# Low parts of weight tiles by accumulating transfers, in the plain stage of a two-layer decoder trunk

## The chip, the cores and the metric

The kernel runs on one core of a Trainium2 chip. The metric is the time of one execution on the device in microseconds (us). Of the kernel before, three timed runs are shown; their median is 888.7 us. A profiled execution of the same program gives the rows that are quoted here: for each engine when an instruction started, how long it took and what ended the idle time ahead of it. The engines are called as the profile calls them: PE is the matrix engine's multiplying, PEld its loading of weights, DVE the vector engine, ACT the scalar engine, POOL the general engine (GpSimd), SP the engine that here only issues transfers. POOL can issue transfers too.

## The reference

Two layers over 512 tokens of width 1024, in float32. Layer 0 mixes tokens with causal means over 2, 4, 8 and 16 tokens, layer 1 with sliding-window attention. Behind each mixer stands a gated MLP with a causal convolution of width 3 over the tokens:

```python
def conv_glu_ffn(h, w_in, conv_w, conv_b, w_out):
    u = h @ w_in
    c = lax.conv_general_dilated(u, conv_w[:, None, :], window_strides=(1,),
        padding=[(CONV_W - 1, 0)], dimension_numbers=('NWC', 'WIO', 'NWC'),
        feature_group_count=2 * D_FF) + conv_b
    a, g = c[..., :D_FF], c[..., D_FF:]
    return (a * jax.nn.silu(g)) @ w_out
```

D_FF is 2816, so w_in is 1024 by 5632. RMS norms stand ahead of mixers and MLPs and at the end.

## The kernel before, in words

Every product of float32 matrices is made of three products of a shorter format, float32r: an operand x is split into a high part, x rounded to float32r, and a low part, the rest x - high, also float32r; high by high, high by low and low by high are added up in one accumulation bank. `mm3` (lines 89 to 91) issues the three. For a weight tile of 128 by 1024, `weights` (line 98 on) fetches the raw tile by SP, makes the high part by an ACT copy (line 105) and the low part by a subtraction (line 108), on DVE or, for layer 0's first MLP stage, on POOL in four pieces of 256 columns. Raw tiles lie in a ring of three buffers, high and low parts in rings of four each; a fetch waits until the last reader of the buffer three tiles ago is through, a split until PE has finished with the tile four ago.

The program begins with products of zeros on PE (`warm`, line 257), while the first inputs arrive. Then come the pooling mixer (line 290: means over tokens as products with a band matrix `sband`, which DVE scales at line 288) and layer 0's MLP, `mlp_halves`. Its 22 blocks of 128 features come in two kinds. The first seven are "plain": for each block j and each side s (1 the gate, 0 the value) one chunk, 24 products of 512 columns on the weight tile wi_j_s, 14 chunks in all. The other 15 blocks, the halves stage, are made with fewer products from sums and differences of weights (`uw_...` tiles: r, u, v and q) and of the two halves of the input (`th`, `tl`), which DVE and ACT prepare during the plain stage (lines 413 to 433). Between their products PE does the down projection piece by piece (`down`), in two banks that take turns; DVE adds each finished piece to h (line 533), and PE may write the bank again only after that.

For a chunk, DVE scales the finished bank (line 395), ACT and DVE make the convolution's three taps (359, 360, 361), ACT the gate's silu (372), DVE the product of gate and value (376), and both split it (390, 391). Chunks' jobs are put off by some chunks and handed out by a short table of letters per chunk. uw_u tiles are summed by a transfer from memory and a second, accumulating one on POOL's queue (line 451); uw_v comes from two POOL sums (487, 488).

Which instruction stands where in an engine's list is set by the tile framework, which orders the recorded work by its own estimate of when things are ready, save where a pin keeps the written order; each engine then works its list strictly in order. `pre` has the first four weight tiles, which are split during the mixer, by `early_weights`. The loop over the remaining twelve chunks starts a tile's load one chunk ahead:

```python
ahead = [load(2)]
for at in range(2, len(todo)):
    w, ps = ahead.pop(0), chunk(at)
    for i in {11: (12, 13), 12: ()}.get(at, (at + 1,)):
        ahead.append(load(i))
```

Of the kernel before, what the change touches and what calls it, by code (L numbers as in the profile page):

```python
# [19 lines left out]
F32 = mybir.dt.float32  # L20
F32R = mybir.dt.float32r
I32 = mybir.dt.int32
AF = mybir.ActivationFunctionType
ALU = mybir.AluOpType
AX = mybir.AxisListType

P = 128
D = 1024
# [34 lines left out]
def trunk(ctx: ExitStack, tc: tile.TileContext, x_tok, x_t, vecs, w_pool, w_kq, w_v, w_o, gain, w_in, w_half, w_down, w_tok, out):  # L63
    nc = tc.nc
    V, A, G, T = nc.vector, nc.scalar, nc.gpsimd, nc.tensor
# [3 lines left out]
    wp = ctx.enter_context(tc.tile_pool(name="wp", bufs=4))  # L69
# [12 lines left out]
    def bank(tag):  # L82
        rings[tag].append(rings[tag].pop(0))
        return banks[rings[tag][-1]]


    def mm3(ps, w, x, start, stop, **kw):
        (wh, wl), (xh, xl) = w, x
        T.matmul(ps, lhsT=wh, rhs=xh, start=start, stop=False, **kw)  # L89
        T.matmul(ps, lhsT=wh, rhs=xl, start=False, stop=False, **kw)  # L90
        T.matmul(ps, lhsT=wl, rhs=xh, start=False, stop=stop, **kw)  # L91

    def fetch(src, n, name):
        raw = wp.tile([P, 1024], F32, tag="raw", name=f"{name}_raw", bufs=3)
        nc.sync.dma_start(raw[:, :n], src)
        return raw
# [3 lines left out]
    def weights(src, n, name, eng=None, raw=None, step=1024, pin=lambda ins: ins):  # L100

        raw = raw or fetch(src, n, name)
        h = wp.tile([P, 1024], F32R, tag="wh", name=f"{name}_h")
        l = wp.tile([P, 1024], F32R, tag="wl", name=f"{name}_l")
        pin(A.activation(h[:, :n], raw[:, :n], AF.Copy))  # L105
        for a in range(0, n, step):
            o = slice(a, min(a + step, n))
            lows.append((eng or V).tensor_tensor(l[:, o], raw[:, o], h[:, o].bitcast(F32), ALU.subtract))  # L108
        return h, l

    def part(w, k, m=P):
        return tuple(t[:, k * m : (k + 1) * m] for t in w)

    def in_weights(layer, j, s, eng=None, raw=None, pin=lambda ins: ins):
        return weights(w_in[layer][j, s], D, f"wi{layer}_{j}_{s}", eng, raw, 256 if eng else 1024, pin)
# [23 lines left out]
    h = [hp[c // 2][:, (c % 2) * S : (c % 2 + 1) * S] for c in range(NC)]  # L139
# [17 lines left out]
    for g, w in enumerate(WINDOWS):  # L157
# [5 lines left out]
        f = band[:, 4 + g, : w - 1]  # L163
# [86 lines left out]
    def pool_mixer(norm, xs, ws):  # L250
# [2 lines left out]

        warm = small(fst, BW, 192, name="warm")
        V.memset(warm, 0.0)
        for i in range(12):
            T.matmul(banks[-1][:, :BW], lhsT=warm[:, :P], rhs=warm, start=True, stop=True)  # L257
        for i in range(NT):

# [2 lines left out]
            if cut < D:  # L262
                for g in range(2):
# [6 lines left out]
                        scale=1.0,  # L270
# [93 lines left out]
    def mlp_halves(fp, xs, norm, ws0, after):  # L364
# [39 lines left out]
        def spread_signs():  # L404
            mx, px = (sm.tile([P, S], F32, tag="sq", name=f"{x}x") for x in "mp")
            A.activation(mx[:, lo], rb[:, lo], AF.Copy, scale=-1.0)
            A.activation(mx[:, hi], rb[:, hi], AF.Copy)
            A.activation(px, mx, AF.Copy, scale=-1.0)
            return mx, px
# [6 lines left out]
        def first_part(p):  # L416
            th.append(fp.tile([P, 7, HS], F32R, tag="th", name=f"th{p}", bufs=4))
            tl.append(fp.tile([P, 7, HS], F32R, tag="tl", name=f"tl{p}", bufs=4))
            y = spare(p, f"ty{p}").bitcast(F32).rearrange("p (a b) -> p a b", a=4)
            ys.append(y)  # L420
            m2, p2 = (blocks(t) for t in signs)
            V.scalar_tensor_tensor(y[:, 0:4:3, :], blocks(h[p]), col(V_NFF + p), m2, ALU.mult, ALU.mult)  # L422
            V.scalar_tensor_tensor(y[:, 1:3, :], blocks(h[p + 4]), col(V_NFF + p + 4), p2, ALU.mult, ALU.mult)
            split_part(y, p, 0, 3)

        def second_part(p):
            y = ys[p]
            v = spare(p + 4, f"tv{p}").bitcast(F32).rearrange("p (a b) -> p a b", a=4)
            tv.append(v)
            V.tensor_tensor(v[:, 0, :], y[:, 3, :], y[:, 2, :], ALU.add)  # L430
            V.tensor_tensor(v[:, 1, :], y[:, 3, :], y[:, 0, :], ALU.add)
            V.scalar_tensor_tensor(v[:, 2, :], y[:, 2, :], -1.0, v[:, 1, :], ALU.mult, ALU.subtract)
            V.tensor_tensor(v[:, 3, :], y[:, 1, :], v[:, 2, :], ALU.subtract)
            split_part(v, p, 3, 7)
# [11 lines left out]
        def fetch_sums(j):  # L446

            src = w_half[j - PLAIN]
            u = us[j] = fp.tile([P, 1024], F32, tag="ur", name=f"uw{j}_u_raw", bufs=2)
            nc.sync.dma_start(blocks(u), src[:, 0:4:2, :])  # L450
            pin(G.dma_start(blocks(u), src[:, 2:4, :], accum_op=ALU.add))

        def fetch_rows(j):

            if j > PLAIN:
                rs[j] = wp.tile([P, 1024], F32, tag="raw", name=f"uw{j}_r_raw", bufs=3)
            else:
                rs[j] = fp.tile([P, 1024], F32R, tag="vh", name=f"uw{j}_r_raw", bufs=3).bitcast(F32)
            nc.sync.dma_start(blocks(rs[j]), w_half[j - PLAIN][:, 0:2, :])
# [3 lines left out]
        def keep():  # L463
            hold.append(tuple(wp.tile([P, 1024], F32R, tag=f"w{k}", name=f"uw_hold{len(hold)}_{k}") for k in "hl"))
# [8 lines left out]
        def first_weights(j):  # L473

            if j > PLAIN:
                q = wp.tile([P, 1024], F32, tag="raw", name=f"uw{j}_q_raw", bufs=3)
            else:
                q = sm.tile([P, S], F32, tag="sq", name=f"uw{j}_q_raw")
            nc.sync.dma_start(q[:, :half], w_half[j - PLAIN][:, 3, :])
            raws[j] = q  # L480
            uw[j] = kept((j - PLAIN) % 2, slice(0, 1024), rs[j]), own_split(us[j], f"uw{j}_u")
# [32 lines left out]
        def down_split(i):  # L514
            if i < len(steps):
                g, m = steps[i]
                n = DOWN0[g] * P
                at, a = (2, half) if i % 3 == 0 else (3, i % 3 * half - half)
                w = kept(at, slice(a, a + n), down_raw.pop(i)[:, :n])
                down_w[i] = [part(w, k) for k in range(DOWN0[g])]  # L520
# [24 lines left out]
        todo = [(j, s) for j in range(PLAIN) for s in (1, 0)]  # L545
        jobs, ends, fetched = [], [], 0

        def work(n=1, *more):
            for x in range(min(n, len(jobs))):
                f, *args = jobs.pop(0)  # L550
                f(*args, *more)

        def load(i):
            if i < len(todo):
                return ws0.pop(0) if ws0 else in_weights(0, *todo[i], G)

        def chunk(i):
            if i == 6:
                rings["ps"][:0] = [6, 7]
            ps = bank("ps")  # L560
            jobs.append((late, *todo[i], ps))
            return ps

        w, pss = [load(i) for i in range(2)], [chunk(i) for i in range(2)]
        for k in range(NC):
            for i in range(2):
                mm3(pss[i], part(w[i], k), xs[k], k == 0, k == NC - 1)
        ahead = [load(2)]
        for at in range(2, len(todo)):
            w, ps = ahead.pop(0), chunk(at)  # L570
            for i in {11: (12, 13), 12: ()}.get(at, (at + 1,)):
                ahead.append(load(i))
            for k in range(NC):
                if at == 3 and k == 3:
                    r = norm.stats(bank("aux"), root=True)
                if at == 3 and k == 6:
                    rb = norm.spread(r)
                    signs = spread_signs()
                mm3(ps, part(w, k), xs[k], k == 0, k == NC - 1)
            for x in {3: "01", 4: "01", 5: "01", 6: "01", 7: "21f", 8: "21f", 9: "21", 10: "21gd", 11: "1rd", 12: "ea", 13: "vg"}.get(at, ""):  # L580
                if x == "0":
                    first_part(len(th))
                elif x == "2":
                    second_part(len(tv))
                elif x == "1":
                    work()
                elif x == "f":
                    fetch_sums(PLAIN + fetched)
                    fetched += 1
                elif x == "r":  # L590
                    keep()
                    keep()
                    hold.insert(1, None)
                    first_weights(PLAIN)
                    down_split(0)
                elif x == "g":
                    fetch_rows(PLAIN + (at > 12))
                elif x == "a":
                    add_weights(PLAIN)
                elif x == "d":  # L600
                    down_fetch(at - 10)
                elif x == "e":
                    work(1, ends)
                else:
                    summed = second_weights(PLAIN, pin)
# [428 lines left out]
    ws0 = []  # L1034
# [7 lines left out]
    with tc.tile_pool(name="ap", bufs=2) as ap:  # L1042
# [150 lines left out]
        todo = work()  # L1193
# [187 lines left out]
```

## Time and profile before

| | us |
|---|---|
| three timed runs | 888.65, 888.7, 890.28 |
| median | 888.7 |
| profiled execution | 889.68 |
| its span, first to last instruction | 887.8 |
| PE busy | 876.8 |
| DVE busy | 703.1 |
| ACT busy | 509.5 |
| POOL busy | 251.9 |

A row of a timeline holds the start, the duration, the engine, the source line, the operation, the tile written and the tiles read, the shape and a count of merged instructions, and, in brackets, the idle time just before with what ended it. A row of a group holds the busy time of all its instructions and the mean of one in ns. A row of stretches holds the busy time of each engine in that stretch. Matrix products overlap: a row's duration is longer than the distance to the next, and the distance is what counts. The plain stage runs from about 27 to 103 us, the halves stage from there to about 350.

### The profile page before, as it was taken

The page shows a single profiled execution, that of the slowest core. Times are in us where ns is not written, and L with a number is a line of the kernel's source. Part 1 is how long each engine was busy: PE and PEld are TensorE (multiplying, and loading weights), DVE is VectorE, ACT ScalarE, POOL GpSimd, SP SyncE. Part 2 cuts the span into 40 slices and gives each one's busy share as a digit, 9 for nine tenths or more (in the row PEclk, how much of TensorE's full clock was granted, in tenths as well). Part 3 has the DMA queues.
Part 4 walks back from the last instruction along what each step waited for, and adds up shares of the span by engine and source line. Part 5 has one row for each costly group of instructions (what it writes and reads, how often), then busy time and mean ns, then how long its engine had stood idle before and what let it go on. Part 6 is the DMA issues. An engine that isn't in the chain of part 4 may idle for free.

```text
span 887.8 us, 12919 instructions
## 1 busy us (share of the span) xinstructions
PE 876.8 (99%) x4720; PEld 760.2 (86%) x4720; DVE 703.1 (79%) x1106; ACT 509.5 (57%) x851; POOL 251.9 (28%) x331
## 2 busy tenths in 40 slices
PE   8999999999999999999999999999999999999996
PEld 8888889999999998888899888888888888888885
DVE  7989998887788885765887386998886777876887
ACT  7856555645455553545888375797633444533644
POOL 4767332221313110345765130000230002200122
PEclk9999999999999999999999999999999999999999
DMA  8444346565555543222110042265386231582423
GB/s 324 143 137 122 109 128 183 152 166 145 145 163 153 133 131 88 80 85 103 52 48 25 1 142 95 99 165 163 77 205 217 95 95 48 118 229 89 133 61 105
DMA packets 38559, 109.98 MB, mean 124 GB/s; under 512 B 4064, under 2 KB 6112, under 8 KB 38496
## 3 DMA queue, kind: packets, MB, share of 16 engines
q1 hardware_dynamic: 34464, 95.26, 33.0%
q0 software_dynamic: 3888, 13.63, 9.3%
q8 instruction: 37, 0.61, 0.3%
q10 hardware_dynamic: 144, 0.26, 0.1%
q14 instruction: 26, 0.21, 0.1%
HBM read 107.04 MB, written 2.10 MB: 123 GB/s over the span
## 4 chain that ended last, share of the span: by engine, by line
PE 87%; DVE 9%; ACT 2%; issue 1%; POOL 0%; ACTq 0%; DVEq 0%
PE bank L89 28%; PE bank L90 28%; PE bank L91 28%; PE bank L1217 1%; PE bank L1245 1%; ACT sc L1233 1%; DVE bank L395 1%; PE bank L290 1%; DVE tl L414 1%; PE bank L257 1%; DVE uw_hold_l L470 1%; DVE a_t L376 1%; DVE a_t L361 0%; DVE g_t L360 0%; DVE ty L422 0%
## 5 line engine op out<-in xcount | busy, mean ns | idle before, releaser
L89 PE MATMUL bank<-f1x_h,wi_h 128*128 128x512 f32 x352 | 137.1, 389 | 0.0
L90 PE MATMUL bank<-f1x_l,wi_h 128*128 128x512 f32 x352 | 136.9, 389 | 0.0
L91 PE MATMUL bank<-f1x_h,wi_l 128*128 128x512 f32 x352 | 136.8, 389 | 0.0
L105 ACT ACTIVATE wi_h<-wi_raw 128x1024 fp32r<-128x1024 f32 x58 | 61.4, 1058 | 59.0 <-PE bank L90 41.0
L108 DVE TENSOR_TENSOR wi_l<-wi_raw,wi_h 128x1024 fp32r<-128x1024 f32 x44 | 53.8, 1222 | 37.3 <-ACT wi_h L105 37.1
L91 PEld LDWEIGHTS bank<-f1x_h,wi_l 128*128 128x128 f32 x352 | 66.1, 188 | 14.0 <-DVE wi_l L108 0.2
L90 PEld LDWEIGHTS bank<-f1x_l,wi_h 128*128 128x128 f32 x352 | 66.1, 188 | 13.7
L89 PEld LDWEIGHTS bank<-f1x_h,wi_h 128*128 128x128 f32 x352 | 66.1, 188 | 13.5
L487 POOL TENSOR_TENSOR uw_r_raw<-uw_r_raw,uw_u_raw 128x512 f32<-128x512 f32 x15 | 25.1, 1670 | 162.6 <-DVE uw_hold_l L470 149.8
L108 POOL TENSOR_TENSOR wi_l<-wi_raw,wi_h 128x256 fp32r<-128x256 f32 x56 | 53.5, 987 | 28.5 <-ACT wi_h L105 28.4
L844 POOL TENSOR_TENSOR wt_a_raw<-wt_a_raw,wt_s_raw 128x1024 f32<-128x1024 f32 (+1 forms) x6 | 13.4, 2235 | 144.6 <-DVE wt_a_l L108 142.3
L91 PE MATMUL bank<-th,uw_hold_l 128*128 128x256 f32 x180 | 50.9, 283 | 0.0
L90 PE MATMUL bank<-tl,uw_hold_h 128*128 128x256 f32 x180 | 50.9, 283 | 0.0
L89 PE MATMUL bank<-th,uw_hold_h 128*128 128x256 f32 x180 | 50.8, 282 | 0.0
L832 POOL DMA_DIRECT2D wt_s_raw<-w_tok x12 | 10.5, 871 | 140.8 <-DMA wt_s_raw<-w_tok 86.8
L222 POOL TENSOR_TENSOR n_acc<-n_acc,n_sq 128x512 f32<-128x512 f32 x13 | 19.1, 1470 | 86.4 <-ACT n_sq L213 86.3
L90 PE MATMUL bank<-f0x_l,wi_h 128*128 128x512 f32 x112 | 43.6, 389 | 0.0
L91 PE MATMUL bank<-f0x_h,wi_l 128*128 128x512 f32 x112 | 43.6, 389 | 0.0
L89 PE MATMUL bank<-f0x_h,wi_h 128*128 128x512 f32 x112 | 43.0, 390 | 0.0
L469 ACT ACTIVATE uw_hold_h<-wo_raw 128x512 fp32r<-128x512 f32 (+1 forms) x48 | 28.4, 591 | 25.3 <-PE bank L90 18.8
L533 DVE TENSOR_TENSOR h<-bank,h 128x512 f32<-128x512 f32 x48 | 32.9, 685 | 11.7 <-PE bank L91 11.4
L689 ACT ACTIVATE c_t<-bank,vec 128x512 f32<-128x512 f32 x44 | 33.4, 766 | 8.3 <-PE bank L91 5.3
(440 smaller groups left out, 2825.3 us busy)
## 6 DMA issues: line engine op xcount, KB each, us to landing
wi_raw<-w_in SPq DMA_DIRECT2D x58, 512.0 KB, 3.3
wo_raw<-w_down SPq DMA_DIRECT2D x32, 256.0 KB, 2.6
uw_u_raw<-w_half SPq DMA_DIRECT2D x15, 512.0 KB, 5.5
uw_u_raw<-w_half POOLq DMA_DIRECT2D x15, 512.0 KB, 5.8
uw_r_raw<-w_half SPq DMA_DIRECT2D x15, 512.0 KB, 3.4
wt_a_raw<-w_tok SPq DMA_DIRECT2D x15, 512.0 KB, 3.9
wt_s_raw<-w_tok SPq DMA_DIRECT2D x11, 512.0 KB, 4.0
kq_raw<-w_kq SPq DMA_DIRECT2D x10, 512.0 KB, 3.2
```

Source lines behind the costliest of these rows:

```text
L89: T.matmul(ps, lhsT=wh, rhs=xh, start=start, stop=False, **kw)
L90: T.matmul(ps, lhsT=wh, rhs=xl, start=False, stop=False, **kw)
L91: T.matmul(ps, lhsT=wl, rhs=xh, start=False, stop=stop, **kw)
L105: pin(A.activation(h[:, :n], raw[:, :n], AF.Copy))
L108: lows.append((eng or V).tensor_tensor(l[:, o], raw[:, o], h[:, o].bitcast(F32), ALU.subtract))
L222: eng.tensor_tensor(self.acc[:, lo:hi], self.acc[:, lo:hi], sq[:, lo:hi], ALU.add)
L469: A.activation(w[0], raw, AF.Copy)
L487: G.tensor_tensor(r[:, :n], r[:, :n], u[:, n:], ALU.add)
L533: V.tensor_tensor(h[m], ps, h[m], ALU.add)
L689: taps.append(A.activation(t, ps, AF.Identity, bias=col(V_CB + layer * 2 * NF + m), scale=cw[2]))
L832: pin(G.dma_start(r[:, :n], src[:, b1, :], accum_op=ALU.add))
L844: G.tensor_tensor(r[:, :n], r[:, :n], raws["s1", s][:, :n], ALU.add)
```

## The change

Three edits. A new function, `landed_weights`, takes the place of `in_weights` for layer 0's tiles from the fifth on (ten tiles: the first four come from `pre`). It fetches the raw tile and makes the high part as before. Then ACT copies the raw tile a second time with scale -1 into the low tile, which rounds it to minus the high part, and a transfer on POOL's queue adds the raw tile to it where it lies, from on-chip memory to on-chip memory. Raw minus high is the low part, as before. The raw buffer is read until that transfer has landed. Second, two tiles are loaded ahead in the loop, and the special cases at 11 and 12 are gone. Third, ten calls with zeros are made at the start where there were twelve; each is two instructions in the profile, so 20 for 24.

```diff
+    def landed_weights(layer, j, t):
+
+        raw = fetch(w_in[layer][j, t], D, f"wi{layer}_{j}_{t}")
+        h = wp.tile([P, 1024], F32R, tag="wh", name=f"wi{layer}_{j}_{t}_h")
+        l = wp.tile([P, 1024], F32R, tag="wl", name=f"wi{layer}_{j}_{t}_l")
+        A.activation(h, raw, AF.Copy)
+        A.activation(l, raw, AF.Copy, scale=-1.0)
+        G.dma_start(l.bitcast(F32), raw, accum_op=ALU.add)
         return h, l
...
-        for i in range(12):
+        for i in range(10):
             T.matmul(banks[-1][:, :BW], lhsT=warm[:, :P], rhs=warm, start=True, stop=True)
...
-                return ws0.pop(0) if ws0 else in_weights(0, *todo[i], G)
+                return ws0.pop(0) if ws0 else landed_weights(0, *todo[i]) if i > 2 else in_weights(0, *todo[i], G)
...
-        ahead = [load(2)]
+        ahead = [load(2), load(3)]
         for at in range(2, len(todo)):
             w, ps = ahead.pop(0), chunk(at)
-            for i in {11: (12, 13), 12: ()}.get(at, (at + 1,)):
-                ahead.append(load(i))
+            ahead.append(load(at + 2))
```

POOL's list in the plain stage, before. The names are wi_j_s, and l, h and raw are the low, high and raw tile; x4 are the four pieces.

```order
L108 TENSOR_TENSOR wi_1_0_l<-wi_1_0_raw,wi_1_0_h 128x256 x4
L108 TENSOR_TENSOR wi_2_1_l<-wi_2_1_raw,wi_2_1_h 128x256 x4
L108 TENSOR_TENSOR wi_2_0_l<-wi_2_0_raw,wi_2_0_h 128x256 x4
L108 TENSOR_TENSOR wi_3_1_l<-wi_3_1_raw,wi_3_1_h 128x256 x4
L108 TENSOR_TENSOR wi_3_0_l<-wi_3_0_raw,wi_3_0_h 128x256 x4
L108 TENSOR_TENSOR wi_4_1_l<-wi_4_1_raw,wi_4_1_h 128x256 x4
L451 DMA uw_u_raw<-w_half 128x1024
L108 TENSOR_TENSOR wi_4_0_l<-wi_4_0_raw,wi_4_0_h 128x256 x4
L451 DMA uw_u_raw<-w_half 128x1024
L108 TENSOR_TENSOR wi_5_1_l<-wi_5_1_raw,wi_5_1_h 128x256 x4
```

The same stretch of POOL's list with the change (the lines below the new function move by ten, or nine):

```order
L108 TENSOR_TENSOR wi_1_0_l<-wi_1_0_raw,wi_1_0_h 128x256 x4
L118 DMA wi_2_1_l<-wi_2_1_raw 128x1024
L118 DMA wi_2_0_l<-wi_2_0_raw 128x1024
L118 DMA wi_3_1_l<-wi_3_1_raw 128x1024
L118 DMA wi_3_0_l<-wi_3_0_raw 128x1024
L118 DMA wi_4_1_l<-wi_4_1_raw 128x1024
L118 DMA wi_4_0_l<-wi_4_0_raw 128x1024
L461 DMA uw_u_raw<-w_half 128x1024
L118 DMA wi_5_1_l<-wi_5_1_raw 128x1024
L461 DMA uw_u_raw<-w_half 128x1024
L118 DMA wi_5_0_l<-wi_5_0_raw 128x1024
```

Forty subtractions have gone and ten transfers stand in their places; the two accumulations of uw_u come one tile later.

ACT's list around the first changed tile, before:

```order
L213 ACTIVATE n_sq_472<-h_98 128x512
L105 ACTIVATE wi_2_1_h<-wi_2_1_raw 128x1024
L213 ACTIVATE n_sq_475<-h_99 128x512
L213 ACTIVATE n_sq_478<-h_99 128x512
L105 ACTIVATE wi_2_0_h<-wi_2_0_raw 128x1024
L105 ACTIVATE wi_3_1_h<-wi_3_1_raw 128x1024
L184 ACTIVATE rs_y<-bank_76,eps 128x16
```

And with the change:

```order
L223 ACTIVATE n_sq_470<-h_98 128x512
L116 ACTIVATE wi_2_1_h<-wi_2_1_raw 128x1024
L223 ACTIVATE n_sq_473<-h_99 128x512
L223 ACTIVATE n_sq_476<-h_99 128x512
L117 ACTIVATE wi_2_1_l<-wi_2_1_raw 128x1024
L116 ACTIVATE wi_2_0_h<-wi_2_0_raw 128x1024
L117 ACTIVATE wi_2_0_l<-wi_2_0_raw 128x1024
L116 ACTIVATE wi_3_1_h<-wi_3_1_raw 128x1024
L117 ACTIVATE wi_3_1_l<-wi_3_1_raw 128x1024
L194 ACTIVATE rs_y<-bank_76,eps 128x16
```

Each tile's negated copy stands behind its high copy, for this tile behind two squares of the norm as well; the high copies keep their places among ACT's other work. In SP's list the fetch of wi_6_1's raw tile now stands behind two fetches of the halves stage (a down-projection tile and a uw_q tile) instead of ahead of them. On DVE one split of uw_u moves up by eight places at the end of the plain stage, and three operations beside it change places; PE's list is the same but for the zeros.

More of the change, by code (lines that the diff above doesn't have):

```diff
@@ L108, in weights @@
             lows.append((eng or V).tensor_tensor(l[:, o], raw[:, o], h[:, o].bitcast(F32), ALU.subtract))
+        return h, l
+    def landed_weights(layer, j, t):
[5 more added lines that the diff above has]
+        G.dma_start(l.bitcast(F32), raw, accum_op=ALU.add)
         return h, l
```

## The prediction

> **What bounds the kernel now.** I read the page first (busy time, chain, groups), then the stretches in which the changed code runs, then the idle time of TensorE by place. The whole kernel is a TensorE program:
>
> ```profile
> span 887.8 us, 12919 instructions
> PE 876.8 (99%) x4720; PEld 760.2 (86%) x4720; DVE 703.1 (79%) x1106; ACT 509.5 (57%) x851; POOL 251.9 (28%) x331
> 60.00:104.00 44.00, 44.00 (x198) 36.53 (x197) 43.93 (x65) 24.66 (x31) 28.04 (x26) 1.00 0.46 128
> ```
>
> PE is busy 876.8 of 887.8 us, so the change can only win what lies in the other 11 us, or what PE spends on the zero products. The third row is the plain stage (columns: stretch and its length, then PE, PEld, DVE, ACT, POOL busy, granted clock, DMA share, GB/s). PE has no idle time in it, yet DVE has none either: 43.93 of 44. So making low parts faster earns nothing inside the stage; the question is what a DVE that has lagged all through it costs afterwards. The timeline of PE shows one stall, 15 us behind the stage's end:
>
> ```profile
> 118.09 0.39 PE L91 MATMUL bank<-z2h,uw_hold_l 128*128 128x512 f32 x1
> 119.45 0.50 PE L89 MATMUL bank<-z0h,uw_hold_h 128*128 128x512 f32 x1 [0.97 <-DVE h L533]
> 119.79 0.40 PE L90 MATMUL bank<-z0l,uw_hold_h 128*128 128x512 f32 x1
> 60.48 0.39 PE L89 MATMUL bank<-f0x_h,wi_h 128*128 128x512 f32 x1
> 60.94 0.39 PE L91 MATMUL bank<-f0x_h,wi_l 128*128 128x512 f32 x1
> ```
>
> Undisturbed products follow each other by 0.23 us (60.48 to 60.94 is two steps). From 118.09 to 119.45 are 1.36, and the restart takes 0.34: 1.13 + 0.11 = **1.24 us** lost, because a down-projection product wants a bank that DVE's add (h, L533) has not read out. Why that add is late is in DVE's and ACT's timelines:
>
> ```profile
> 104.69 1.89 DVE L395 TENSOR_TENSOR bank<-bank,n_rb 128x512 f32<-128x512 f32 x3
> 104.96 0.38 ACT L633 ACTIVATE sn<-bank 128x256 f32<-128x256 f32 x1 [1.83 <-PE bank L91]
> 107.35 1.05 ACT L469 ACTIVATE uw_hold_h<-uw_r_raw 128x1024 fp32r<-128x1024 f32 x1
> 109.60 1.22 DVE L470 TENSOR_TENSOR uw_hold_l<-uw_r_raw,uw_hold_h 128x1024 fp32r<-128x1024 f32 x1
> 110.89 2.21 POOL L487 TENSOR_TENSOR uw_r_raw<-uw_r_raw,uw_u_raw 128x512 f32<-128x512 f32 x1 [8.87 <-DVE uw_hold_l L470]
> 118.72 0.68 DVE L533 TENSOR_TENSOR h<-bank,h 128x512 f32<-128x512 f32 x1
> ```
>
> DVE works its list without a gap; the add stands 9.12 us behind uw_hold_l, whose input ACT had ready at 107.35 + 1.05 = 108.40 while DVE came at 109.60. DVE is 1.2 us late there.
>
> **The change part by part.** *What leaves DVE's way.* Ten weight tiles lose their four POOL subtractions. While those run, some DVE operations take half a microsecond more:
>
> ```profile
> 70.82 3.90 POOL L108 TENSOR_TENSOR wi_l<-wi_raw,wi_h 128x256 fp32r<-128x256 f32 x4 [1.15 <-ACT wi_h L105]
> 72.01 1.23 DVE L376 TENSOR_TENSOR a_t<-a_t,g_t 128x512 f32<-128x512 f32 x1
> 118.12 0.68 DVE L376 TENSOR_TENSOR a_t<-a_t,g_t 128x512 f32<-128x512 f32 x1
> L422 DVE SCALAR_TENSOR_TENSOR ty<-h,vec,mx 128x512 f32<-128x512 f32 x4 | 4.3, 1092 | 0.0
> L423 DVE SCALAR_TENSOR_TENSOR ty<-h,vec,px 128x512 f32<-128x512 f32 x4 | 5.0, 1255 | 0.0
> L360 DVE SCALAR_TENSOR_TENSOR g_t<-bank,vec,g_t 128x511 f32<-128x511 f32 x5 | 3.7, 737 | 0.0
> L376 DVE TENSOR_TENSOR a_t<-a_t,g_t 128x512 f32<-128x512 f32 x4 | 3.8, 953 | 0.0
> L430 DVE TENSOR_TENSOR tv<-ty 128x256 f32<-128x256 f32 x4 | 2.2, 546 | 0.0
> L433 DVE TENSOR_TENSOR tv<-ty,tv 128x256 f32<-128x256 f32 x4 | 2.2, 545 | 0.0
> L432 DVE SCALAR_TENSOR_TENSOR tv<-ty,tv 128x256 f32<-128x256 f32 x4 | 1.6, 410 | 0.0
> ```
>
> The groups are those of 49 to 98 us. Against 0.74 for a product-and-add of this width that reads a bank (L360), 0.68 for L376 beside no POOL work, and 0.41 for the 256-wide ones: L422 4 x 0.35, L423 4 x 0.52, L376 4 x 0.27, L430 and L433 8 x 0.14. That is 1.4 + 2.1 + 1.1 + 1.1 = **5.7 us** less work for DVE before 98. It is an estimate: L422 and L423 read other tiles than L360, so part of theirs may be their own.
>
> *What of it reaches PE.* Not 5.7. DVE then catches up with its inputs and waits. At the first halves block the inputs come by way of sn, whose row shows ACT waiting 1.83 us for PE; after it ACT is busy without a break until uw_hold_h ends. So uw_hold_l gains the 1.2 us by which DVE was late and what PE itself gains earlier, and no more. The add at 118.72 gains the same 1.2; PE's wait of 1.13 goes but for some 0.05, as POOL's sum at 110.89 moves along and may stretch another DVE operation. With the restart I take **1.2 us**; ends: 0, if DVE is held at another place before 109, and 1.24.
>
> *The zero products.* 24 instructions become 20, in front of the first real product:
>
> ```profile
> 2.23 5.92 PE L257 MATMUL bank<-warm 128*128 128x144 f32 x24 [2.23 <-DVE warm L255]
> 7.67 0.48 PE L257 MATMUL bank<-warm 128*128 128x144 f32 x2
> 7.99 7.83 PE L290 MATMUL bank<-sband,xt 128*128 128x144 f32 x64
> 6.87 0.37 DVE L288 TENSOR_SCALAR sband<-band,r 128x288 f32<-128x288 f32 x1
> 7.67 0.42 DVE L288 TENSOR_SCALAR sband<-band,r 128x288 f32<-128x288 f32 x1
> ```
>
> The first 22 take (7.67 - 2.23) / 22 = 0.25 us each, the real ones 7.83 / 64 = 0.12: the pitch halves at about 7.7, though the granted clock of these rows is 1.00. Twenty leave PE free at about 7.2; the first half of sband is written at 7.24, the second at 8.09, in time for the ninth product. So real products start near 7.3 instead of 7.99, two or three of them at the slow pitch: gain 0.7 - 2.5 x 0.12 = **0.4 us** (ends 0 and 0.7). It survives to the end, as PE then waits only for what PE's own products release.
>
> *The added work.* Ten ACT copies with scale -1 and ten accumulating transfers on POOL's queue:
>
> ```profile
> 38.68 1.05 ACT L105 ACTIVATE wi_h<-wi_raw 128x1024 fp32r<-128x1024 f32 x1
> 48.92 0.39 PE L89 MATMUL bank<-f0x_h,wi_h 128*128 128x512 f32 x1
> 86.65 1.05 ACT L105 ACTIVATE wi_h<-wi_raw 128x1024 fp32r<-128x1024 f32 x1
> 97.88 0.39 PE L89 MATMUL bank<-f0x_h,wi_h 128*128 128x512 f32 x1
> 61.39 1.03 POOL L451 DMA_DIRECT2D uw_u_raw<-w_half  x1
> wi_raw<-w_in SPq DMA_DIRECT2D x58, 512.0 KB, 3.3
> uw_u_raw<-w_half POOLq DMA_DIRECT2D x15, 512.0 KB, 5.8
> DMA to landing us min/median/max: 3.6/6.0/8.7
> ```
>
> ACT: 10 x 1.05 = 10.5 us on an engine that is busy 24.66 of 44; none of them waits for anything that the high copy ahead of it does not, so what queues behind them (gates, splits) is late by at most one copy. I cost them at nothing; the cover is ACT's waiting for DVE. The nearest row for the transfer is the accumulation of uw_u, of the same 512 KB but from memory: 5.8 us median from issue, POOL's 0.9 to 1.0 included, 8.7 at worst. The first changed tile (fifth chunk) has its high copy at 38.68; behind it stand two squares and then the negated copy, which ends near 41.7, so the low part lands at 47.5, or 50.4 at worst. Its first use is the third product of the chunk, 48.92 + 0.45 = 49.4. The last tile: 86.65 + 2.1 = 88.7, lands at 94.5 or 97.4, used at 98.3. So at the median it costs nothing, with 1.9 and 3.8 us of slack; at the worst only the fifth chunk is late, by 1.0.
>
> A raw tile is now held until the transfer lands. One of the three raw buffers then goes through fetch 3.3, two copies 2.1 and transfer 5.8, about 11 us with nothing in between, against 3 chunks of 24 x 0.227 = 5.44, 16.3 us. SP's exchange of the raw tile of (6, 1) with two fetches of the halves stage moves them past a wait, not behind one. POOL's sums for the halves stage stand behind the last transfer's issue at 88.7; the first of them starts at 97 now. Loading "two chunks ahead" buys little beyond that: the high copies keep their places among ACT's other work.
>
> **Sum.** Against the profiled execution's span 887.8: -1.2 - 0.4 = 886.2. That execution's own time is 889.68, 1.9 around the span, and the three timed runs have a median of 888.7; the difference of 1.6 is taken from the median: **887.1 us**, 0.18% less. About 0.2%, 1.8 us, is what a measurement of this kernel can tell from no change, so the forecast lies just inside.
>
> **Rivals.** *The whole gain and more* (DVE's relief ends the stall outright, and the start yields its 0.7): 1.24 + 0.7 gives 886.8. For it: the 5.7 us are five times what is needed; against: ACT's unbroken run after sn. *The start gives nothing*: the slow pitch may end earlier in another execution; had it ended 1 us sooner, the 24 products would have been through by 7.3, when sband is ready anyway. Then 1.2 alone: 887.5. The Trainium skill ("TensorE: Matmul & The Clock Gate", Part 1: The HAM clock gate) says that the window that releases the clock is free-running, about 3.4 us long, so that the number of slow products varies between executions of the same kernel; by that rule the start's 0.4 would be only one draw, and no trace here shows another. *The stall stays*: DVE is held before 109 by something else, for one by ACT's ten copies; then only the start's 0.4: 888.3. *Slower: the low parts come late.* Mechanism: the landing of one transfer releases SP's next fetch, which then shares the DMA engines with the next transfer, and two uw_u accumulations stand in the same POOL queue. It decides where the landing passes 8.9 us, because 3.3 + 2.1 + 2 of queueing on ACT + 8.9 is the 16.3 of three chunks. At 9.5 us each round of three chunks loses 0.6, over the ten tiles 2.0, and the fifth chunk 41.7 + 9.5 - 49.4 = 1.8; less the 1.6 gained: 890.9. At 11 the same sum gives 897. I price it at 891. For it: 8.7 is in the row above; against: that was beside two fetches of 512 KB, and the DMA share is 0.46 here. *The change does not relieve DVE*: if the long L422 and L423 are their own, 2.2 us remain, still more than 1.2; so this is no case of its own.
>
> **How the numbers follow.** Forecast 887.1: 0.52. Whole gain 886.8: 0.14. Start gives nothing 887.5: 0.11. Stall stays 888.3: 0.10. Low parts late 891: 0.13. The bound of 0.2% is at 886.9: some two fifths of the forecast's share lie under it (its own range is 886.5 to 887.7), 0.20, and of the whole gain's 0.11: faster 0.31. Slower by over 0.2% is the late case: 0.13. The rest, 0.56, is no change. The range of 8 in 10 reaches from 886.4 over the cases up to 888.3 into the mildest of the late case: 886.4 to 889.4.
>
> **What would show it.** In the profile after: L376, L422, L423, L430 and L433 at 0.68, 0.74 and 0.41 in 50 to 98; DVE idle there; uw_hold_l within 0.2 us of uw_hold_h's end; no PE wait for h L533 near 118; the first L290 at 7.3; the new transfers landing in 5 to 7 us and no PE wait for wi_l. Wrong it would be if PE waits inside the plain stage, if the long DVE rows stay long, or if the stall only moves behind 120.

## The result: slower, and the profile after

The changed kernel takes 894.6 us (median of 6 runs, 894.0 to 895.7) against 889.15 for the kernel before (6 runs, 888.65 to 890.28): a ratio of 1.0060, 95% interval 1.0047 to 1.0073. That is 5.5 us slower, where 887.1 was forecast and 889.4 was the upper end of the range. The profiled execution has a span of 893.2 us against 887.8, so the 5.4 us of loss are in the trace. (Of one variant below, e10, only the time is used, because its profiled execution ran at a granted clock of 0.56.) The first lines of the page of the changed kernel, then its row for the plain stage (columns as in the prediction):

```profile
span 893.2 us, 12903 instructions
PE 877.8 (98%) x4716; PEld 759.3 (85%) x4716; DVE 695.0 (78%) x1106; ACT 517.5 (58%) x861; POOL 221.9 (25%) x301
60.00:104.00 44.00, 41.55 (x175) 33.29 (x174) 36.55 (x60) 30.05 (x38) 7.38 (x9) 0.96 0.86 207
```

POOL has lost its subtractions (7.38 us busy from 60 to 104, 28.04 before), DVE has lost work too (36.55 where it was 43.93), and PE, which had no idle time in this stretch, is busy for only 41.55 of 44. Its clock there is 0.96, and the DMA engines are busy 0.86 of the time, 0.46 before. So the relief came, and something else took more. PE's timeline names the places:

```profile
81.44 0.39 PE L90 MATMUL bank<-f0x_l,wi_h 128*128 128x512 f32 x1
82.36 0.50 PE L91 MATMUL bank<-f0x_h,wi_l 128*128 128x512 f32 x1 [0.54 <-DMA wi_l<-wi_raw]
87.72 0.39 PE L90 MATMUL bank<-f0x_l,wi_h 128*128 128x512 f32 x1
90.01 0.50 PE L91 MATMUL bank<-f0x_h,wi_l 128*128 128x512 f32 x1 [1.91 <-DMA wi_l<-wi_raw]
91.08 0.63 PE L91 MATMUL bank<-f0x_h,wi_l 128*128 128x512 f32 x1
91.51 0.63 PE L89 MATMUL bank<-f0x_h,wi_h 128*128 128x512 f32 x1
115.15 0.39 PE L91 MATMUL bank<-z1h,uw_hold_l 128*128 128x512 f32 x1
116.49 0.39 PE L89 MATMUL bank<-th,uw_u_h 128*128 128x256 f32 x1 [0.95 <-ACT sn L659]
123.43 0.39 PE L91 MATMUL bank<-z2h,uw_hold_l 128*128 128x512 f32 x1
124.80 0.50 PE L89 MATMUL bank<-z0h,uw_hold_h 128*128 128x512 f32 x1 [0.98 <-DVE h L543]
```

Start to start, less the pitch of 0.23 and with 0.11 for each restart, the pauses cost 0.8 us at 81.4, 2.2 at 87.7, 1.2 at 115.2 and 1.3 at 123.4. After the pause at 87.7 eight products follow each other by 0.43 instead of 0.23 (91.08 to 91.51), which is another 1.6. Together 7.1 (a first wait of 0.2 us, at 70.3, is left out). The stall of 1.24 at 118 in the profile before is the last of them under a new time, and the first real product started 0.7 us earlier, of which 0.55 is left at the first product of the weights (15.26 for 15.81). 7.1 - 1.24 - 0.55 = 5.3 of the 5.4 us.

Why the low parts came late stands in the chain of waits, in order of time (start, duration, what):

```profile
41.76 6.14 DMA wi_l<-wi_raw
47.96 6.39 DMA wi_raw<-w_in
54.46 1.06 ACT wi_h L116
...
72.47 9.85 DMA wi_l<-wi_raw
```

The transfer into the low part of the fifth chunk's tile is issued at 41.76 and lands after 6.14 us. Until then it holds its raw tile, one of three. Only at 47.96 may SP fetch the eighth chunk's tile into that buffer, and the fetch takes 6.39 us where 3.3 is its median before. ACT has the copy of that tile (wi_h, 54.46) at the head of its list, ahead of px, which the next block of DVE's work needs. The timelines of ACT and DVE show the wait being handed on:

```profile
54.46 1.06 ACT L116 ACTIVATE wi_h<-wi_raw 128x1024 fp32r<-128x1024 f32 x1 [5.99 <-DMA wi_raw<-w_in]
56.08 0.75 DVE L433 SCALAR_TENSOR_TENSOR ty<-h,vec,px 128x512 f32<-128x512 f32 x1 [5.65 <-ACT px L418]
79.29 1.06 ACT L116 ACTIVATE wi_h<-wi_raw 128x1024 fp32r<-128x1024 f32 x1 [3.82 <-DMA wi_raw<-w_in]
72.50 0.69 DVE L386 TENSOR_TENSOR a_t<-a_t,g_t 128x512 f32<-128x512 f32 x1
73.11 0.42 DVE L443 TENSOR_TENSOR tv<-ty,tv 128x256 f32<-128x256 f32 x1
```

ACT stands still for 6 us and DVE for 5.7. No product waits for it yet, and ACT catches up: its high copies come 4.1, 3.0, 1.5 and 0.5 us later than before (54.46 for 50.38, 59.69 for 56.69, 65.46 for 63.96, 70.18 for 69.68). The fetches do not, since each of them waits for a landing. The twelfth chunk's tile is the one that costs most. Its fetch, before and with the change, and how long the fetch and the tile's own transfer (issued at 81.59) took with the change:

```profile
61.47 0.33 SPq L95 DMA_DIRECT2D wi_raw<-w_in  x1
70.66 0.33 SPq L95 DMA_DIRECT2D wi_raw<-w_in  x1
wi_raw<-w_in SPq DMA_DIRECT2D x1, 512.0 KB, 8.6
wi_l<-wi_raw POOLq DMA_DIRECT2D x1, 512.0 KB, 8.4
```

The fetch is issued 9.2 us later than before, when the ninth chunk's transfer has landed at 70.6, and it takes 8.6 us. ACT waits for it (79.29) and copies at once, the transfer takes 8.4 us, and PE can go on at 90.01. From the fetch to the landing that is 19.3 us, where the prediction had about 11 for this sum and 16.3 to spend. In the last rows of the timelines above stands the relief: L386 (L376 before) at 0.69, L443 (L433 before) at 0.42, as foreseen.

The fetches are slow as well as late, the first one (47.96) already. Two stretches of the DMA engines around it, by queue (packets, MB, share of 16 engines), 47.9 to 51.2 us in the first row, 51.2 to 54.5 in the next two, and POOL's timeline ahead of them:

```profile
q0 software_dynamic: 159, 0.59, 109.0%
q1 hardware_dynamic: 270, 1.01, 75.6%
q0 software_dynamic: 34, 0.07, 18.5%
41.76 1.05 POOL L118 DMA_DIRECT2D wi_l<-wi_raw  x1 [3.62 <-ACT wi_l L117]
...
45.47 0.86 POOL L118 DMA_DIRECT2D wi_l<-wi_raw  x1 [0.99 <-ACT rs_y L194]
```

In the first 3.3 us behind the fetch's issue only packets of the software queue move, those of the accumulating transfers that POOL issued between 41.76 and 45.47; the hardware queue's row is missing there and appears in the second stretch. So two causes offer themselves: the raw tile that is **held** until a transfer lands, and the DMA engines that the transfers **fill**. Two more have to be ruled out: the ten added copies on ACT, and PE's own waiting for the landed low parts.

### The profile page after: what moved, and what is told of

It is laid out like the page before. It is cut to its first block, busy times and chain, and to the rows that moved or that the text cites. A ratio compares the mean times of both kernels' runs of the same rounds, so it can differ in the third digit from the quotient of the medians.

```text
span 893.2 us, 12903 instructions
## 1 busy us (share of the span) xinstructions
PE 877.8 (98%) x4716; PEld 759.3 (85%) x4716; DVE 695.0 (78%) x1106; ACT 517.5 (58%) x861; POOL 221.9 (25%) x301
## 4 chain that ended last, share of the span: by engine, by line
PE 88%; DVE 5%; DMA 3%; ACT 2%; issue 1%; DVEq 0%; ACTq 0%; SPq 0%
PE bank L89 28%; PE bank L91 28%; PE bank L90 28%; DMA wi_l<-wi_raw 2%; PE bank L1226 1%; PE bank L1254 1%; PE bank L300 1%; DMA wi_raw<-w_in 1%; DVE uw_hold_l L480 1%; ACT sc L1242 1%; DMA uw_r_raw<-w_half 1%; DVE bank L405 0%; DMA xt<-x_tok 0%; ACT th L423 0%; DVE tl L424 0%
## 5 line engine op out<-in xcount | busy, mean ns | idle before, releaser
L105 ACT ACTIVATE wi_h<-wi_raw 128x1024 fp32r<-128x1024 f32 x48 | 50.9, 1061 | 56.9 <-PE bank L90 37.0
L91 PEld LDWEIGHTS bank<-f1x_h,wi_l 128*128 128x128 f32 x352 | 66.1, 188 | 14.1 <-DVE wi_l L108 0.2
L91 PE MATMUL bank<-th,uw_hold_l 128*128 128x256 f32 x180 | 50.9, 283 | 0.0
L90 PE MATMUL bank<-tl,uw_hold_h 128*128 128x256 f32 x180 | 50.9, 283 | 0.0
L853 POOL TENSOR_TENSOR wt_a_raw<-wt_a_raw,wt_s_raw 128x1024 f32<-128x1024 f32 (+1 forms) x6 | 13.4, 2236 | 144.3 <-DVE wt_a_l L108 142.0
L480 DVE TENSOR_TENSOR uw_hold_l<-wo_raw,uw_hold_h 128x512 fp32r<-128x512 f32 (+1 forms) x48 | 36.6, 763 | 1.7 <-ACT uw_hold_h L479 1.7
```

The costliest lines, as they stand in the source:

```text
L480: V.tensor_tensor(w[1], raw, w[0].bitcast(F32), ALU.subtract)
L853: G.tensor_tensor(r[:, :n], r[:, :n], raws["s1", s][:, :n], ALU.add)
```

## The experiments

All times are medians of 11 timed runs (e8: 5, e10: 12, the changed kernel: 6), each ratio against the kernel before on the same chip, whose medians were 889.15, 888.89 and 889.14 in the three groups. A sentence first on what such a difference can tell: e4 and e7 turned out to be one and the same list of instructions, and they stand at 889.58 and 890.28; e1 and e12 are one kernel, at 888.41 and 889.16. Differences of less than about 0.8 us between groups are therefore not read here, only what the traces show.

| run | what | us | ratio, 95% interval |
|---|---|---|---|
| changed kernel | | 894.62 | 1.0060 (1.0047 to 1.0073) |
| e1 | before, ten zero products | 888.41 | 0.9991 (0.9982 to 1.0000) |
| e2 | no low parts for ten tiles | 888.13 | 0.9990 (0.9981 to 0.9998) |
| e3 | copies, no transfers | 889.32 | 1.0002 (0.9994 to 1.0011) |
| e4 | transfers read HBM | 889.58 | 1.0002 (0.9993 to 1.0011) |
| e5 | every second tile lands | 889.93 | 1.0010 (1.0001 to 1.0019) |
| e6 | transfers of half the size | 888.39 | 0.9993 (0.9984 to 1.0002) |
| e7 | as e4 | 890.28 | 1.0014 (1.0005 to 1.0023) |
| e8 | low parts not read | 903.50 | 1.0164 (1.0150 to 1.0177) |
| e9 | two more raw buffers | 888.48 | 0.9993 (0.9984 to 1.0002) |
| e10 | e4, from the sixth chunk | 888.38 | 0.9992 (0.9983 to 1.0001) |
| e11 | half landed, half subtracted | 889.87 | 1.0009 (1.0000 to 1.0017) |
| e12 | as e1 | 889.16 | 0.9998 (0.9989 to 1.0007) |

### The parts without the transfers: e1, e2, e3

```
e1  -        for i in range(12):          (kernel before)
    +        for i in range(10):
e2  -        A.activation(l, raw, AF.Copy, scale=-1.0)
    -        G.dma_start(l.bitcast(F32), raw, accum_op=ALU.add)
    -        return h, l
    +        return h, h
e3  -        G.dma_start(l.bitcast(F32), raw, accum_op=ALU.add)
```

> The kernel before with ten zero products at the start in place of twelve, nothing else. In the profile of the changed kernel the chain through the first 45 us stands 0.56 us earlier than before. Theory (the low parts' transfers hold the raw tiles, so that a fetch comes late): the start is a gain of its own, 0.4 to 0.6 us below the kernel before. Rival (the start gives nothing, what was won there is lost at the next wait): within 0.2 us of the kernel before.

> The changed kernel without the negated copies and without the transfers for its ten tiles: the low parts are left out, and TensorE multiplies the high part a second time in their place, so that its work is the same. Nothing but the one copy on ScalarE is left on those tiles, two chunks ahead. Theory (the fetch comes late because of the transfers): the sum of the prediction should stand here, 1.2 to 1.8 us below the kernel before. Rival (two chunks ahead, or the end of the stage, does the harm): slower than before by over 2 us here as well. Rival (relief of VectorE reaches TensorE nowhere): 0.4 to 0.6 us below the kernel before, as the ten zero products alone.

> The changed kernel with both copies on ScalarE and without the transfers: the low part of the ten tiles stays the negated high part, so the sum of the raw tile is left out. Theory (the transfers do the harm, not the copies): as without low parts at all, 1.0 to 1.8 us below the kernel before. Rival (the ten added copies, 1.06 us each, hold up ScalarE's list): slower than before by 2 to 5 us.

None of the three shows a loss: neither the order two chunks ahead nor the ten copies cost what the change cost. In the trace of e3 PE loses nothing between 45 and 117 us, as in e2; its median is 1.2 above e2's, but where no copy stands: the first product of the weights starts 0.6 later (15.50 for 14.89), and the output leaves 0.9 later behind DVE's last operation (more on that end below). The rival that the copies hold up ACT's list (2 to 5 us) is out. In e3 the two accumulations of uw_u moved up to 38 us, and three fetches beside them took 7.8 to 9.2 us; they had been issued by 44.89, and no product waited for them.

e2 is also the test of the prediction's own sum, since nothing in it is late. It stands 1.0 us below the kernel before (0.2 to 1.7), just short of what was expected, and its trace says which term is missing. From e2, DVE and ACT ahead of the stall:

```profile
103.98 0.38 ACT L639 ACTIVATE sn<-bank 128x256 f32<-128x256 f32 x1 [8.81 <-PE bank L91]
104.92 0.69 DVE L398 TENSOR_TENSOR z4l<-a_t,z4h 128x512 fp32r<-128x512 f32 x1 [1.67 <-ACT z4h L397]
106.38 1.05 ACT L476 ACTIVATE uw_hold_h<-uw_r_raw 128x1024 fp32r<-128x1024 f32 x1
108.04 1.22 DVE L477 TENSOR_TENSOR uw_hold_l<-uw_r_raw,uw_hold_h 128x1024 fp32r<-128x1024 f32 x1
116.95 0.39 PE L91 MATMUL bank<-z2h,uw_hold_l 128*128 128x512 f32 x1
117.89 0.50 PE L89 MATMUL bank<-z0h,uw_hold_h 128*128 128x512 f32 x1 [0.56 <-DVE h L540]
```

DVE is so far ahead here that it waits, 1.67 us, for ACT's z4h, and ACT waits 8.81 for PE. From z4l on DVE works five operations of 3.1 us, and comes to uw_hold_l at 108.04, 0.6 behind its input (106.38 + 1.05 = 107.43). So half of the lateness that the prediction saw at this place is not inherited from the plain stage; it is DVE's own list since sn, and no relief before 98 can shorten it. The stall shrinks from 1.24 to 0.82 (0.94 from start to start, less 0.23, with 0.11), and in e1, with all of POOL's subtractions still there and DVE busy for 49.00 of 49 us, it is 0.84. So no gain of DVE is seen on PE.

### Hold or sharing: e4, e7, e10

```
e4  -        G.dma_start(l.bitcast(F32), raw, accum_op=ALU.add)
    +        G.dma_start(l, w_in[layer][j, t].bitcast(F32R), accum_op=ALU.add)
e7  e4, and  -  landed_weights(...) if i > 2     +  ... if i > 3
e10 e4, and  -  landed_weights(...) if i > 2     +  ... if i > 4
```

> The changed kernel with the accumulating transfers reading the weights a second time from HBM in place of the raw tile in SBUF: the transfers are as many and as large, but the raw tile is free as soon as ScalarE has copied it. Theory A (the raw tile that is held till the landing makes SP's next fetch late): most of the loss goes, 886.5 to 890 us. Theory B (the transfers fill the DMA engines, and a fetch lands late because its packets wait, whoever holds the tile): 892 to 896 us, and the fetches land after 5 us and more where they took 3.4 before.

> The kernel whose transfers read the weights from HBM, with GpSimd subtracting for one tile more, the fourth chunk's, for which TensorE waited 1.48 us: nine tiles land. Theory A (the raw tile's hold is all that costs, beside that one wait): 887.7 to 888.7 us, as the kernel without low parts. Theory B (transfers that share the DMA engines cost in the whole stage): 889.2 us or more.

> The kernel whose transfers read the weights from HBM, with GpSimd subtracting for the fifth chunk's tile too, whose low part TensorE waited 1.5 to 1.7 us for: nine tiles land. (The run with nine tiles sent before, by its list of instructions, was the kernel with ten again: the fourth chunk's tile is loaded ahead of the stage.) Theory A: the one wait goes and no other comes, 887.9 to 889 us. Theory B (sharing): 889.2 us or more.

e4 moves the same number of accumulated bytes over the same queue, but the raw tile is free after ACT's two copies. Five of the 5.5 us are gone. The views of DMA issues from 38 to 100 us (KB each, median us to landing), of the kernel before, the changed kernel and e4 in this order:

```profile
wi_raw<-w_in SPq DMA_DIRECT2D x8, 512.0 KB, 3.3
wi_l<-wi_raw POOLq DMA_DIRECT2D x10, 512.0 KB, 6.6
wi_raw<-w_in SPq DMA_DIRECT2D x8, 512.0 KB, 5.8
wi_l<-w_in POOLq DMA_DIRECT2D x10, 512.0 KB, 10.0
wi_raw<-w_in SPq DMA_DIRECT2D x7, 512.0 KB, 6.6
```

In e4 the fetches and the landings are both slower than in the changed kernel (6.6 for 5.8, 10.0 for 6.6), and yet only one product in the stage waits:

```profile
48.04 0.39 PE L90 MATMUL bank<-f0x_l,wi_h 128*128 128x512 f32 x1
49.75 0.50 PE L91 MATMUL bank<-f0x_h,wi_l 128*128 128x512 f32 x1 [1.32 <-DMA wi_l<-w_in]
```

That is the fifth chunk's low part, 1.71 us from start to start. e7 was meant to take just this tile out, and by its list of instructions took out none: the first four chunks' tiles are loaded ahead of the stage, so the condition began one tile too early. It is a second run of e4, with a PE wait of the same kind (1.65 us above the pitch, 1.88 from start to start). At 890.28 it lies above theory B's bound of 889.2, but since it is e4 over again, that decides nothing. e10 takes the tile out, and 888.38 is where theory A put it. Theory B (sharing costs in the whole stage) is out here, where the fetches are issued early.

### The hold itself: e9

```
+    def landed_weights(layer, j, t, own=None):
+        if own is None: raw = fetch(...)
+        else:
+            raw = own.tile([P, 1024], F32, tag="ur", ..., bufs=2)
+            nc.sync.dma_start(raw, w_in[layer][j, t])
+    ... landed_weights(0, *todo[i], fp if i in (5, 8) else None) if i > 2 ...
```

> The changed kernel with two more buffers for raw tiles in the first half of the stage: the raw tiles of the sixth and the ninth chunk stand in the two buffers that later take the sums of the composed features (whose first fetches come later for it), all else, the transfers from SBUF above all, as in the changed kernel. Theory A (the hold of the raw tile in a ring of three): the late fetch at 48 us and ScalarE's wait for it (5.99 us) go, and with them most of the loss, 888 to 891 us. Theory B (the transfers' share of the DMA engines): the fetches land as late as before, 892 to 895 us.

e9 leaves the transfers as the change has them, from the raw tiles. The two stretches of 49 to 98 us, of the changed kernel and of e9, and e9's DMA issues in 38 to 100:

```profile
49.00:98.00 49.00, 46.55 (x196) 37.43 (x195) 36.85 (x61) 33.19 (x41) 7.79 (x9) 0.97 0.84 200
49.00:98.00 49.00, 49.00 (x218) 40.58 (x217) 42.36 (x68) 35.83 (x45) 8.09 (x10) 1.00 0.93 228
wi_l<-wi_raw POOLq DMA_DIRECT2D x10, 512.0 KB, 6.4
wi_raw<-w_in SPq DMA_DIRECT2D x6, 512.0 KB, 5.2
```

The DMA engines are busier than in the changed kernel, 0.93 for 0.84, the transfers land after 6.4 us for 6.6 and the fetches after 5.2 for 5.8, and PE is busy for 49.00 of 49. The slowest landing is even slower, 11.5 us for 9.8:

```profile
DMA to landing us min/median/max: 4.8/6.4/11.5
```

ACT still waits 3.81 us for a fetch, but for the thirteenth chunk's tile, which it copies at 78.71 and not at 87.66. 888.48 us: the whole loss is gone with two buffers, given to two of the ten tiles. The hold of the raw tile in a ring of three is shown as the cause. The slow fetches and landings that come with sharing make the hold longer, and by themselves they cost nothing here. One thing beside the buffers differs in e9: SP fetches the halves of the composed features' sums later (50.9 and 63.2 us), as they wait for those buffers.

### How long the hold may be: e5, e6, e11

```
e5  -  landed_weights(...) if i > 2
    +  landed_weights(...) if i > 2 and i % 2 == 0
e6  -        G.dma_start(l.bitcast(F32), raw, accum_op=ALU.add)
    +        G.dma_start(l[:, :512].bitcast(F32), raw[:, :512], accum_op=ALU.add)
e11 e6 with the copy of the left half only, and for the right half
    +        for o in (slice(512, 768), slice(768, 1024)):
    +            G.tensor_tensor(l[:, o], raw[:, o], h[:, o].bitcast(F32), ALU.subtract)
```

> The changed kernel with the landing low parts for every second tile only (the fifth, seventh, ... chunk, five tiles in place of ten); GpSimd subtracts for the others, as before. Theory A (a raw tile that is held for 7 to 12 us in a ring of three makes the next fetch late): with only one of two neighbouring tiles held so long, the ring has slack again, 888 to 890.5 us. Rival (each landing costs its own 0.5 us, wherever it stands): half of the loss stays, 891 to 892.5 us.

> The changed kernel with transfers of half the size: only the left 512 of the 1,024 columns of each tile are accumulated, 256 KB in place of 512; the right half of the low part stays the negated high part, so its raw values are left out. Theory A (length of the hold): the raw tile comes free some 2 to 4 us sooner, and most of the loss goes, 888 to 891 us. Rival (that the raw tile is released by a transfer's landing at all, by its fixed time, is what costs): over 892 us.

> A whole computation again: of each of the ten tiles ScalarE and a transfer of 256 KB make the left half of the low part, and GpSimd subtracts the right half. Theory A: the raw tiles come free in time, as with the transfers of half the size alone, 888 to 889.2 us; half of VectorE's relief is kept, and by the runs without low parts that is worth 0.3 us at most. Theory B: between that and the changed kernel, 890 us or more.

Both ways of shortening the hold end the loss in the stage: in all three traces PE loses nothing between 45 and 117 us. With transfers of 256 KB (e6) they land after 4.9 us in the median, the fetches after 4.3, and ACT's longest wait for a raw tile is 2.88 us instead of 5.99. The DMA issues of e6 from 38 to 100 us and that row of ACT:

```profile
wi_raw<-w_in SPq DMA_DIRECT2D x8, 512.0 KB, 4.3
wi_l<-wi_raw POOLq DMA_DIRECT2D x10, 256.0 KB, 4.9
80.11 1.06 ACT L116 ACTIVATE wi_h<-wi_raw 128x1024 fp32r<-128x1024 f32 x1 [2.88 <-DMA wi_raw<-w_in]
```

e5 came out at 889.93 as theory A had it, and its rival (891 to 892.5, each landing at its own price) is out. e11, a whole kernel again, missed its range for A by 0.7 us and B's bound by 0.1; its trace has no loss in the stage that e6 has not. Most of the excess stands at the very end, between the end of DVE's last operation and the end of the span, while the output leaves. DVE ends at 882.78 us in e6, 882.71 in e5 and 882.74 in e11, the span at 886.7, 887.6 and 887.6. That is 3.9 us in e6 and 4.9 in e5 and e11. The other traces have the same two values, 4.9 in e3 and e8 and 3.9 in the rest, so this end does not go with the loss in the stage. What makes the output take longer in some kernels was not tried.

### Nobody reads the low parts: e8

```
e8  -        return h, l           (copies and transfers as in the change)
    +        return h, h
```

> The changed kernel with all its copies and transfers, but TensorE multiplies the high part in place of the low one, so that nothing waits for a landing but the tiles' rings; the low part is left out of the result. Theory A (the late fetch of the next raw tile holds ScalarE's list, and with it VectorE and TensorE): the loss stays, 892 to 895 us. Theory C (TensorE waits for the landed low parts themselves, as its weight loads do for 3.6 us in all in the changed kernel's waits): the loss goes, 888 to 889.5 us.

No product waits for a landing, and the kernel is slower still, by 9 us, where theory C had 888 to 889.5. The size fits no theory, and the reason is a side effect of the edit: with no reader for the low parts, the order of ACT's list changed. The negated copies now stand ahead of work that used to be ahead of them, high copies among it, so a late tile holds up more. From e8, two rows of ACT and one of PE:

```profile
76.76 1.06 ACT L117 ACTIVATE wi_l<-wi_raw 128x1024 fp32r<-128x1024 f32 x1 [7.95 <-DMA wi_raw<-w_in]
84.28 1.04 ACT L116 ACTIVATE wi_h<-wi_raw 128x1024 fp32r<-128x1024 f32 x1
85.37 0.79 PE L89 MATMUL bank<-f0x_h,wi_h 128*128 128x512 f32 x1 [4.15 <-ACT wi_h L116]
```

The high copy for which PE waits (84.28) stands behind two negated copies of later tiles, at 76.76 and 83.32, and both had waited for their fetches. So a late fetch can do harm without any PE wait for a low part, and where the copy stands in ACT's list sets the price. Because the list changed, the run does not decide against theory C in the changed kernel, where the pauses at 81.4 and 87.7 are waits for landings; e9 does, whose landings are as slow and cost nothing.

### Does a version beat both? e12

> The kernel before with ten zero products in place of twelve once more, to see whether it beats the kernel before by more than a measurement tells. Theory A (the start is a gain of its own): 0.4 to 0.9 us below the kernel before. Rival (a tie): within 0.2 us.

e12 is a tie, where e1 stood 0.74 us lower than the kernel before with the same instructions. Of the versions that compute everything, e1, e9 and e10 take 6 us less than the changed kernel. None of them beats the kernel before by more than the 0.2% that can be told.

## Why the prediction was wrong, point by point

- **"The added work" failed, and with it the forecast.** Of its parts the ACT copies ("I cost them at nothing") held: in e3 they cost PE nothing in the stage. The landing of the fifth chunk's low part held too, at 47.9 us without a wait. The step that failed is the raw buffer's cycle, "about 11 us with nothing in between", fetch 3.3, copies 2.1 and transfer 5.8, against the 16.3 us of three chunks. In the changed kernel the transfers land after 4.4 to 9.8 us and the fetches after 3.1 to 13.4, and ACT, whose list has the copies among other work, does not always take a tile when it lands. For the twelfth chunk's tile the cycle was 8.6 + 2.3 + 8.4 = 19.3 us, and PE paused there. With two more buffers (e9) the same transfers cost nothing that the trace shows. The prediction's own sign of being wrong, PE waits inside the plain stage, is what came.
- **Why the median was the wrong row.** 5.8 and 3.3 are medians of the kernel before, with a DMA share of 0.46 in the stage. The change raises the share to 0.86, so the transfers are each other's neighbours. The prediction had a worst landing, 8.7, for its check of the first uses and for the rival. But even in the buffer's cycle it gives 3.3 + 2.1 + 8.7 = 14.1, or 16.1 with the rival's 2 us of queueing on ACT, still below 16.3. The fetch, which shares the engines with the same transfers, had to be taken slow as well.
- **The rival "low parts come late" named the mechanism** (the landing releases SP's next fetch, which shares the engines with the next transfer), at 891 with 0.13. Its shape was a little off: it had every round of three chunks lose the same from a point at 8.9 us. What happens is one fetch of 6.4 us that stops ACT for 6 until 54.46 and that the stage absorbs, and one of 8.6 us at 70.66 that it does not. The fifth chunk, which it priced at 1.8, lost nothing. And it priced neither the slow products behind a pause (1.6) nor the waits at 115 and 123 (1.2 more than before).
- **"What leaves DVE's way" was right in kind**: the rows came out at 0.68 to 0.75 and 0.41 to 0.42, and DVE idles in the stage.
- **"What of it reaches PE" was wrong by its whole size**: 1.2 taken, nothing seen. In e2, with the relief and without any delay, the stall is 0.82, as in e1 without the relief. The step read "DVE is 1.2 us late there" as a debt from the plain stage. In e2, half of it (0.6) is DVE's own operations between sn and uw_hold_l, and the other half is missing in e1 as well (108.16 against 107.55), whose POOL still subtracts. The lower end of 0, "if DVE is held at another place before 109", is what happened.
- **"The zero products" is not settled.** The first product of the weights starts at 15.26 in the changed kernel, 15.03, 14.89, 15.50, 14.73 and 15.25 in e1, e2, e3, e4 and e12, 15.81 before; but 15.68 in e7, and the medians of e1 and e12 lie 0.75 apart. So the trace has 0.1 to 1.1 us, around the forecast's 0.4, and the times can't tell it from nothing. The profiles show why it varies: the slow pitch of the start ends at another time in each. The kernel before (24 products), e1 and e7 (20 each):

```profile
2.23 5.92 PE L257 MATMUL bank<-warm 128*128 128x144 f32 x24 [2.23 <-DVE warm L255]
2.23 4.14 PE L257 MATMUL bank<-warm 128*128 128x144 f32 x20 [2.23 <-DVE warm L255]
2.23 5.17 PE L267 MATMUL bank<-warm 128*128 128x144 f32 x20 [2.23 <-DVE warm L265]
```

The same twenty products take 4.14 us in one execution and 5.17 in another. The Trainium skill's rule that the prediction weighed ("TensorE: Matmul & The Clock Gate", Part 1: The HAM clock gate), a free-running window, agrees: the time from the first product to the full pitch is not a property of the kernel. Where the start was fast, the chain led to another place: in e1 to the landing of vec, 9.27 us after its issue, whose first user on DVE stands ahead of the pooling weights' low parts.

## What to carry to other kernels

A transfer that takes over an engine's work also takes over that work's buffers: the source is held until the landing, so count the buffer's whole cycle with the slowest fetch and the slowest landing that the trace shows rather than the medians, and ask which fetch waits for it and what queues behind that fetch's reader. Where the cycle was too long here, two more buffers (e9), a source that nobody waits for (e4, e10) or a transfer of half the size (e6, e11) each ended the loss in the stage, but for one wait in e4. Before crediting an engine's relief to the end of the program, look whether its list right ahead of the critical wait begins with a wait for the critical engine, as it did in e2: then a lag from before is not inherited.

## What the runs showed of the hardware

- A pause of PE of 2.29 us from start to start (87.72 to 90.01) was followed by some 3 us of products at a pitch of 0.43 in place of 0.23, and one of 4.53 us in e8 likewise (0.63 us for a product's row in place of 0.39, up to 88.1). The first cost 1.6 us beyond the wait. Pauses of 1.88 us in e7, 1.71 in e4 and 1.37 and 1.34 in the changed kernel were followed by the full pitch at once. The length of one pause does not decide alone: in e8, pauses of 1.75, 1.72 and 1.17 us within 6 us (111.4 to 117.1) were followed by some 5 us of products of 256 columns at 0.21 us in place of 0.12. The Trainium skill ("TensorE: Matmul & The Clock Gate", Part 1: The HAM clock gate) has the half clock come after an idle window of about 3.4 us; here a single pause of 2.29 us was enough.
- Beside three accumulating transfers on the software queue a fetch on the hardware queue waited for its turn. In the 3.3 us from 47.9 the software queue's packets took all the time of the 16 engines, and the fetch issued then landed after 6.39 us, where 3.3 is the median before.
